# Putting the up product of a feed-forward pair together in PSUM, with its loads and splits placed earlier

## The chip, the core and the metric

The kernel runs on one core of one Trainium2 chip. The metric is the time of one execution on the device, in microseconds (us); lower is better. Several executions are timed and their median is given, and one further execution is profiled. The engines are named as the profile names them: PE (TensorE; PEld is its weight load), DVE (VectorE), ACT (ScalarE), POOL (GpSimd) and SP (SyncE, which here only issues DMAs).

## The reference

Two layers of an encoder over 512 positions of width 1024, in 32-bit floats. Each layer has a mixer (latent attention beside a gated convolution), then a gated MLP with a depthwise convolution of width 3 between its up product and the SiLU, then a gated embedding. The change is in the MLP:

```python
h = rmsnorm(x, g_ffn[i])
u = dwconv(h @ w_up[i], w_ffn_conv[i])
a, val = u[..., :D_FF], u[..., D_FF:]
x = x + (jax.nn.silu(a) * val) @ w_down[i]
```

D_FF is 2816, so `h @ w_up` has 5632 columns. `dwconv` mixes three neighbouring positions of one channel with three weights of its own (its "taps"), zero at both ends.

## The kernel before

Activations of the MLP lie transposed: 128 channels on the partitions, 512 positions along the free axis. Each 32-bit operand of a product is split into a high part (a copy rounded by ACT, `split` or `wsplit`, line 93 or 106) and a low part (the rest, by a DVE subtraction, line 94 or 107), and `mm3` adds three products: high·high (line 101), high·low of the moving side (102) and low·high (103). So each weight tile is loaded by SP into a `raw` buffer, copied by ACT to `wh` (or `vh`) and subtracted by DVE to `wl` (or `vl`).

The feed-forward works in pairs: pair j is one tile of 128 columns of `a` and the matching tile of `val`, in `w_up` tiles 2j and 2j+1. There are 22 pairs in a layer. The first two (`ew`, `eo`) are plain products whose sums stay in four PSUM banks, from which `taps` reads them. The other 20 go through the generator `pair`, which treats the 2x2 blocks (two halves of the positions, two halves of the 1024 input channels, and `a` beside `val`) by a scheme with seven block products of 256 columns in place of eight. Its inputs are sums and differences of blocks: on the moving side the tiles `hf`, `sh`, `sl`, made once per layer on DVE and ACT (lines 580 to 591), on the weight side four POOL subtractions per pair in the two `raw` buffers (lines 614 to 617), after `r0` (blocks b11, b21) has been split as `w0` and the block b22 as `w22` (`vh`, `vl`). After the second of the four, `r1` is split as `w1`; after the fourth, `r0` is split again as `w2`.

`pair` yields between its steps, called s0 to s7 here:

- s0: load `r0`, `r1`; split `w0` and `w22`; the four POOL subtractions
- s1: product y (with `w0`), in the bank "av"
- s2: product x (with `w0`), in a bank "mm"; y is copied to SBUF (`U`) and x + y goes to `C`, an SBUF tile; split `w1`
- s3: product z (with `w1`), in a bank "sc"; split `w2`
- s4: more onto x (with `w2`); x and z are copied to SBUF (`U`, `Z`)
- s5: more onto x (with `w1`); x + Z goes to `C`
- s6: more onto z (with `w22`); z + U goes to `C`
- s7: more onto x (with `w2`); x is copied to `C`; then `taps` on both halves of `C`, and `gated`

Each step's product is twelve matmuls of 256 columns. `taps` is one scaled copy on ACT (line 563) and two multiply-adds on DVE (564, 565); `gated` is the SiLU on ACT (601), a product on DVE (602, `fa` times `fa`) and a split into `gth`, `gtl` (106, 107).

The down product of four finished pairs is cut in eight pieces (`down`): each is twelve matmuls of 512 columns into a bank "tp", with a DVE addition into the residual `xs` (line 539). It loads and splits four `w_down` tiles per four pairs, two ahead of its first piece and two more later.

The main loop interleaves an old pair, a new one and the next one, and the pieces. On PE the order is that of the code (a manual region), and one turn of the loop is: old s4, new s1, piece, old s5, new s2, new s3, piece, old s6, old s7. The other engines are ordered by the framework's scheduler, and each executes its instructions strictly in the order given, so that one that waits holds up all behind it. There are four `raw` buffers, eight each of `wh` and `wl`, two of `vh` and `vl`, and PSUM banks: two "mm", one "av", two "sc", three "tp".

Of the kernel before, what the change touches and what calls it, by code (L numbers as in the profile page):

```python
# [11 lines left out]
F32 = mybir.dt.float32  # L12
# [4 lines left out]
ALU = mybir.AluOpType  # L17
AX = mybir.AxisListType

P = 128  # L20
L = 2
S = 512
# [18 lines left out]
HS = S // 2  # L41
# [19 lines left out]
def encoder_kernel(ctx, tc, x_in, pT, pos, inv, w_a1, w_z, w_g, w_uq, w_ukv, w_au, w_cu, w_o,  # L61
                   w_up, w_down, w_pg, w_ple, b_gate, g_norm, g_lat, g_nope, g_rope, w_conv,
                   w_fconv, out):
    nc = tc.nc
# [7 lines left out]
    hh = cp.tile([P, NT, KD, P], F32R, name="hh")  # L72
    hl = cp.tile([P, NT, KD, P], F32R, name="hl")
# [3 lines left out]
    def psum(tag="mm"):  # L77
        return ps.tile([P, S], F32, tag=tag, name="ps_" + tag, bufs={"mm": 2, "av": 1, "sc": 2, "tp": 3}[tag])
# [5 lines left out]
    def load(src, n=1024):  # L84
        raw = rawtile(n)
        nc.sync.dma_start(raw, src)
        return raw

    def wsplit(raw, n=1024, tag="w"):
        wp, nr, nw = wpool[-1]  # L90
        h = wp.tile([P, n], F32R, tag=tag + "h", name=tag + "h", bufs=nw if tag == "w" else 2)
        lo = wp.tile([P, n], F32R, tag=tag + "l", name=tag + "l", bufs=nw if tag == "w" else 2)
        nc.scalar.copy(h, raw)  # L93
        nc.vector.tensor_sub(lo, raw, h.bitcast(F32))  # L94
        return h, lo
# [4 lines left out]
    def mm3(o, st, mv, start, stop, more=False):  # L100
        nc.tensor.matmul(o, st[0], mv[0], start=start, stop=False, skip_group_check=more)  # L101
        nc.tensor.matmul(o, st[0], mv[1], start=False, stop=False, skip_group_check=more)  # L102
        nc.tensor.matmul(o, st[1], mv[0], start=False, stop=stop, skip_group_check=more)  # L103

    def split(hi, lo, src):
        nc.scalar.copy(hi, src)
        nc.vector.tensor_sub(lo, src, hi.bitcast(F32))  # L107
# [88 lines left out]
    def pool(name, l):  # L196
        cm = tc.tile_pool(name=f"{name}{l}", bufs=1, reuse_waits="tile")
        p = cm.__enter__()
        return p, lambda: cm.__exit__(None, None, None)

    def layer(l, first):
# [67 lines left out]
        def t2(nm):  # L269
            return tmp.tile([P, S], F32, tag="t2", name=nm, bufs=4)  # L270
# [233 lines left out]
        for m in range(KD):  # L504
            gs = []
            for i in range(2):
                w = weight(w_g[l, 2 * m + i])
                o = psum()
# [48 lines left out]
        ff, close_ff = pool("ff", l)  # L557
# [3 lines left out]
        def taps(i, o):  # L561
            a = t2("fa")
            nc.scalar.activation(a, o, AF.Copy, scale=wfc[:, i, 1:2])  # L563
            nc.vector.scalar_tensor_tensor(a[:, 1:], o[:, :-1], wfc[:, i, 0:1], a[:, 1:], ALU.mult, ALU.add)  # L564
            nc.vector.scalar_tensor_tensor(a[:, :-1], o[:, 1:], wfc[:, i, 2:3], a[:, :-1], ALU.mult, ALU.add)  # L565
            return a
# [11 lines left out]
        hf = [ff.tile([P, 2, 4, P], F32, tag="gt", name="hf", bufs=8) for q in quarter]  # L578
        V = nc.vector
        for o, q in zip(hf, quarter):  # L580
            V.tensor_tensor(o, hh[q].bitcast(F32), hl[q].bitcast(F32), ALU.add)
        h11, h12, h21, h22 = hf
        V.tensor_tensor(h22, h22, h21, ALU.add)
        V.tensor_tensor(h21, h21, h11, ALU.subtract)
# [7 lines left out]
        def quart(r, k0):  # L592
            return lambda k: (hh[:, 2 * r:2 * r + 2, k0 + k, :], hl[:, 2 * r:2 * r + 2, k0 + k, :])

        def summed(i):
            return lambda k: (sh[:, i, :, k, :], sl[:, i, :, k, :])
# [3 lines left out]
        def gated(j, u):  # L600
            nc.scalar.activation(u[0], u[0], AF.Silu)
            nc.vector.tensor_tensor(u[1], u[0], u[1], ALU.mult)
            if j % 2 == 0:
                gt[j // 2] = (ff.tile([P, 2, S], F32R, tag="gt", name="gth", bufs=8),
                              ff.tile([P, 2, S], F32R, tag="gt", name="gtl", bufs=8))
            split(gt[j // 2][0][:, j % 2, :], gt[j // 2][1][:, j % 2, :], u[1])

        def pair(j):
            r0, r1 = load(w_up[l, 2 * j]), load(w_up[l, 2 * j + 1])
            b11, b21, b12, b22 = r0[:, :512], r0[:, 512:], r1[:, :512], r1[:, 512:]  # L610
            w0 = wsplit(r0)
            w22 = wsplit(b22, 512, "v")
            g = nc.gpsimd
            g.tensor_tensor(b22, b12, b22, ALU.subtract)  # L614
            g.tensor_tensor(b12, b12, b11, ALU.subtract)  # L615
            g.tensor_tensor(b11, b11, b22, ALU.subtract)  # L616
            g.tensor_tensor(b21, b21, b11, ALU.subtract)
            yield

            def product(o, w, off, mv, first):  # L620
                for k in range(4):
                    c = slice(off + k * P, off + k * P + P)
                    mm3(o, (w[0][:, c], w[1][:, c]), mv(k), first and k == 0, k == 3, not first)

            C = ff.tile([P, 2, S], F32, tag="C", name="C", bufs=2)
            U = ff.tile([P, HS], F32, tag="U", name="U", bufs=2)
            y = psum("av")[:, :HS]
            product(y, w0, 512, quart(0, 4), True)
            yield
            x = psum("mm")[:, :HS]  # L630
            product(x, w0, 0, quart(0, 0), True)
            nc.scalar.copy(U, y)
            V.tensor_tensor(C[:, 0, :HS], x, U, ALU.add)
            w1 = wsplit(r1)
            yield
            z = psum("sc")[:, :HS]
            product(z, w1, 0, summed(0), True)
            w2 = wsplit(r0)
            yield
            product(x, w2, 0, summed(1), False)  # L640
            U = ff.tile([P, HS], F32, tag="U", name="U", bufs=2)
            Z = ff.tile([P, HS], F32, tag="U", name="Z", bufs=2)
            nc.scalar.copy(U, x)
            nc.scalar.copy(Z, z)
            yield
            product(x, w1, 512, quart(1, 0), False)
            V.tensor_tensor(C[:, 1, HS:], x, Z, ALU.add)
            yield
            product(z, w22, 0, summed(2), False)
            V.tensor_tensor(C[:, 1, :HS], z, U, ALU.add)  # L650
            yield
            product(x, w2, 512, quart(1, 4), False)
            nc.scalar.copy(C[:, 0, HS:], x)
            gated(j, [taps(2 * j + i, C[:, i, :]) for i in range(2)])

        def down(j0, j1, after, tags):
            nk = (j1 - j0) // 2

            def tiles(n):
                return [weight(w_down[l, n * (NJ // 2) + j0 // 2 + k]) for k in range(nk)]  # L660

            wt = tiles(0)
            for n in range(2):
                for t in range(NT):
                    yield
                    tk = slice(t * P, (t + 1) * P)
                    o = psum(tags[t % len(tags)])
                    for i in range(2 * nk):
                        h, lo = gt[j0 // 2 + i // 2]
                        wh, wl = wt[i // 2]  # L670
                        c = slice((i % 2) * 512, (i % 2) * 512 + 512)
                        mm3(o, (h[:, i % 2, tk], lo[:, i % 2, tk]), (wh[:, c], wl[:, c]), i == 0, i == 2 * nk - 1)
                    after(t, n, o)
                    if n == 0 and t == 2:
                        nxt = tiles(1)
                if n == 0:
                    wt = nxt
# [3 lines left out]
        def piece():  # L681
            while downs and next(downs[0], downs) is downs:
                downs.pop(0)

        def advance(g, n=1):
            for _ in range(n if g else 0):
                next(g, None)
# [3 lines left out]
        region = tc.manual_schedule(engines={mybir.EngineType.PE})  # L691
        region.__enter__()
        old, new = None, pair(NS)
        advance(new)
        for q in range(NS, NJ + 1):
            nxt = pair(q + 1) if q + 1 < NJ else None
            advance(old)
            advance(new)
            piece()
            advance(old)  # L700
            advance(new, 2)
            advance(nxt)
            piece()
            advance(old, 2)
            if old and q % 4 == 0:
                downs.append(down(q - 4, q, residual, ("tp",)))
            old, new = new, nxt
# [45 lines left out]
    for l in range(L):  # L753
        layer(l, l == 0)
# [79 lines left out]
```

## Time and profile before

| | |
|---|---|
| median of 3 runs | 1644.79 us (1640.87 to 1645.81) |
| the profiled execution | 1645.68 us |
| its span, first to last instruction | 1643.8 us |
| busy in the span | PE 94%, PEld 82%, DVE 71%, ACT 49%, POOL 22% |
| mean granted clock of PE | 0.975 |
| first product of the 20 pairs, first and second layer | at 396 us and 1212 us of the span |

The page gives shares over the whole span; the change touches only the feed-forward of each layer, so that its price is read from views cut to those stretches: the instructions in order of time, the waits of PE, and the windows. A matmul counts as busy until its modelled end, which lies after the start of the next ones; the pace of PE is read from starts.

### The profile page before, as it was taken

The numbers are of one execution on the slowest core, as the hardware profiler recorded it, in microseconds if no ns is written. First come the engines' busy times: TensorE is split into PE (matmuls) and PEld (weight loads), VectorE is DVE, ScalarE is ACT, GpSimd is POOL, SyncE is SP. The second block draws the span as 40 slices with busy tenths as digits, with TensorE's granted clock in tenths as the row PEclk, the third lists the DMA queues.
The fourth block names the chain that finished last, engine by engine and source line by source line (L and its number), as shares of the span: only waits on it lengthen the run. The fifth ranks groups of instructions, "written<-read, shape, count | busy, mean of one in ns | idle before, by whom it ended". The sixth has DMA issues, their size and how long they took to land.

```text
span 1643.8 us, 22339 instructions
## 1 busy us (share of the span) xinstructions
PE 1542.8 (94%) x8776; PEld 1344.5 (82%) x8776; DVE 1162.6 (71%) x1500; ACT 805.0 (49%) x1336; POOL 364.5 (22%) x313
## 2 busy tenths in 40 slices
PE   7999999988899989999989999999788999999998
PEld 6888888868788878887888888888687888888876
DVE  7787543359789898887367775433688889889862
ACT  6588632234444544555264885332345454455541
POOL 2700000003343343411045000000034334343110
PEclk9999999998899999999999999999898999999999
DMA  6220223213223323243042112322222332323411
GB/s 213 73 65 26 84 87 99 79 64 103 78 78 92 113 78 103 78 152 90 21 138 77 39 39 78 102 91 66 79 89 78 91 104 88 103 77 100 152 51 45
DMA packets 41448, 142.32 MB, mean 87 GB/s; under 512 B 5760, under 2 KB 6272, under 8 KB 41344
## 3 DMA queue, kind: packets, MB, share of 16 engines
q1 hardware_dynamic: 41344, 140.90, 27.8%
q8 instruction: 69, 1.13, 0.3%
q14 instruction: 35, 0.29, 0.1%
HBM read 138.78 MB, written 2.10 MB: 86 GB/s over the span
## 4 chain that ended last, share of the span: by engine, by line
PE 43%; DVE 17%; issue 8%; ACT 3%; DMA 3%; POOL 1%; DVEq 0%; ACTq 0%; POOLq 0%; SPq 0%
PE ps_mm L101 6%; PE ps_mm L103 6%; PE ps_mm L102 6%; DVE fa L565 5%; PE ps_sc L103 5%; DVE fa L564 4%; PE ps_sc L101 4%; PE ps_sc L102 4%; DVE wl L94 4%; DMA raw<-in_w_down_dram 3%; PE ps_tp L103 3%; PE ps_tp L101 2%; PE ps_tp L102 2%; ACT wh L93 1%; DVE xs L539 1%
## 5 line engine op out<-in xcount | busy, mean ns | idle before, releaser
L93 ACT CAST wh<-raw 128x1024 fp32r<-128x1024 f32 (+1 forms) x290 | 297.9, 1045 | 393.3 <-PE ps_mm L102 85.1
L94 DVE TENSOR_TENSOR wl<-raw,wh 128x1024 fp32r<-128x1024 f32 (+1 forms) x290 | 372.9, 1290 | 149.9 <-ACT wh L93 148.4
L101 PE MATMUL ps_mm<-hh,wh 128*128 128x256 f32 (+1 forms) x992 | 337.0, 340 | 4.3 <-ACT wh L93 3.2
L103 PE MATMUL ps_mm<-hh,wl 128*128 128x256 f32 (+1 forms) x992 | 332.5, 335 | 5.8 <-DVE wl L94 5.8
L102 PE MATMUL ps_mm<-hl,wh 128*128 128x256 f32 (+1 forms) x992 | 332.4, 335 | 0.0
L103 PEld LDWEIGHTS ps_mm<-hh,wl 128*128 128x128 f32 x992 | 189.0, 191 | 26.4 <-DVE wl L94 6.4
L101 PEld LDWEIGHTS ps_mm<-hh,wh 128*128 128x128 f32 x992 | 189.3, 191 | 24.8 <-ACT wh L93 3.9
L102 PEld LDWEIGHTS ps_mm<-hl,wh 128*128 128x128 f32 x992 | 189.6, 191 | 18.9
L111 POOL TENSOR_SCALAR ms<-ms 128x1 f32<-128x1 f32 (+2 forms) x40 | 14.3, 356 | 750.6 <-ACT junk L130 722.5
L614 POOL TENSOR_TENSOR raw<-raw 128x512 f32<-128x512 f32 x40 | 62.4, 1560 | 427.4 <-DVE vl L94 427.4
L565 DVE SCALAR_TENSOR_TENSOR fa<-C,wfc,fa 128x511 f32<-128x511 f32 x80 | 131.1, 1675 | 0.0
L103 PE MATMUL ps_tp<-wh,gtl 128*128 128x512 f32 x320 | 128.0, 400 | 1.6 <-DVE gtl L107 1.6
L101 PE MATMUL ps_tp<-wh,gth 128*128 128x512 f32 x320 | 128.9, 403 | 0.0
L102 PE MATMUL ps_tp<-wl,gth 128*128 128x512 f32 x320 | 128.6, 402 | 0.0
L564 DVE SCALAR_TENSOR_TENSOR fa<-C,wfc,fa 128x511 f32<-128x511 f32 x80 | 93.9, 1213 | 24.4 <-ACT fa L563 24.4
L103 PE MATMUL ps_sc<-sh,wl 128*128 128x256 f32 x160 | 51.9, 324 | 48.0 <-DVE wl L94 48.0
L103 PEld LDWEIGHTS ps_sc<-sh,wl 128*128 128x128 f32 x160 | 34.5, 216 | 52.2 <-DVE wl L94 52.2
L103 PEld LDWEIGHTS ps_tp<-wh,gtl 128*128 128x128 f32 x320 | 61.5, 192 | 18.1 <-DVE gtl L107 3.3
L101 PEld LDWEIGHTS ps_tp<-wh,gth 128*128 128x128 f32 x320 | 62.1, 194 | 11.7
L102 PEld LDWEIGHTS ps_tp<-wl,gth 128*128 128x128 f32 x320 | 61.7, 193 | 11.4
L615 POOL TENSOR_TENSOR raw<-raw 128x512 f32<-128x512 f32 x40 | 70.1, 1754 | 2.9
L616 POOL TENSOR_TENSOR raw<-raw 128x512 f32<-128x512 f32 x40 | 67.6, 1689 | 10.0 <-issue 3.6
(291 smaller groups left out, 3676.2 us busy)
## 6 DMA issues: line engine op xcount, KB each, us to landing
raw<-in_w_up_dram SPq DMA_DIRECT2D x88, 512.0 KB, 3.7
raw<-in_w_down_dram SPq DMA_DIRECT2D x44, 512.0 KB, 3.7
raw<-in_w_g_dram SPq DMA_DIRECT2D x32, 512.0 KB, 3.6
raw<-in_w_z_dram SPq DMA_DIRECT2D x24, 512.0 KB, 3.8
raw<-in_w_o_dram SPq DMA_DIRECT2D x16, 512.0 KB, 3.7
raw<-in_w_pg_dram SPq DMA_DIRECT2D x16, 512.0 KB, 3.6
raw<-in_w_au_dram SPq DMA_DIRECT2D x8, 512.0 KB, 3.7
raw<-in_w_cu_dram SPq DMA_DIRECT2D x8, 512.0 KB, 3.6
```

The source lines that it names most:

```text
L93: nc.scalar.copy(h, raw)
L94: nc.vector.tensor_sub(lo, raw, h.bitcast(F32))
L101: nc.tensor.matmul(o, st[0], mv[0], start=start, stop=False, skip_group_check=more)
L102: nc.tensor.matmul(o, st[0], mv[1], start=False, stop=False, skip_group_check=more)
L103: nc.tensor.matmul(o, st[1], mv[0], start=False, stop=stop, skip_group_check=more)
L111: nc.gpsimd.tensor_scalar_add(ms, ms, EPS)
L539: nc.vector.tensor_tensor(xs[:, t, c], xs[:, t, c], o, ALU.add)
L564: nc.vector.scalar_tensor_tensor(a[:, 1:], o[:, :-1], wfc[:, i, 0:1], a[:, 1:], ALU.mult, ALU.add)
L565: nc.vector.scalar_tensor_tensor(a[:, :-1], o[:, 1:], wfc[:, i, 2:3], a[:, :-1], ALU.mult, ALU.add)
L614: g.tensor_tensor(b22, b12, b22, ALU.subtract)
L615: g.tensor_tensor(b12, b12, b11, ALU.subtract)
L616: g.tensor_tensor(b11, b11, b22, ALU.subtract)
```

## The change

The sums of a pair no longer go to the SBUF tile `C`. The product x is put in the right half of an "mm" bank (`m0`), and x + y is written by DVE into the left half; z is put in the left half of an "sc" bank (`m1`), x + Z is written into its right half, and z + U is added in place. `taps` then reads `m0` and `m1` in PSUM. The ACT copy of the last x to `C` is gone. Both banks are held until the taps have read them. `U`, `Y` and `Z` share four small SBUF buffers.

The split of `w1` is placed behind s1 instead of s2 and that of `w2` behind s2 instead of s3, and the next pair's s0 now stands between the new pair's s2 and s3. The order of the products on PE is the same. Once per layer, the four additions that make `hf` go from DVE to POOL.

```diff
         for o, q in zip(hf, quarter):
-            V.tensor_tensor(o, hh[q].bitcast(F32), hl[q].bitcast(F32), ALU.add)
+            nc.gpsimd.tensor_tensor(o, hh[q].bitcast(F32), hl[q].bitcast(F32), ALU.add)
...
-            C = ff.tile([P, 2, S], F32, tag="C", name="C", bufs=2)
-            U = ff.tile([P, HS], F32, tag="U", name="U", bufs=2)
+            def side(nm):
+                return ff.tile([P, HS], F32, tag="U", name=nm, bufs=4)
+
             y = psum("av")[:, :HS]
             product(y, w0, 512, quart(0, 4), True)
-            yield
-            x = psum("mm")[:, :HS]
-            product(x, w0, 0, quart(0, 0), True)
-            nc.scalar.copy(U, y)
-            V.tensor_tensor(C[:, 0, :HS], x, U, ALU.add)
             w1 = wsplit(r1)
             yield
-            z = psum("sc")[:, :HS]
-            product(z, w1, 0, summed(0), True)
+            m0 = psum("mm")
+            x = m0[:, HS:]
+            product(x, w0, 0, quart(0, 0), True)
+            Y = side("Y")
+            nc.scalar.copy(Y, y)
+            V.tensor_tensor(m0[:, :HS], x, Y, ALU.add)
             w2 = wsplit(r0)
             yield
+            m1 = psum("sc")
+            z = m1[:, :HS]
+            product(z, w1, 0, summed(0), True)
+            yield
             product(x, w2, 0, summed(1), False)
-            U = ff.tile([P, HS], F32, tag="U", name="U", bufs=2)
-            Z = ff.tile([P, HS], F32, tag="U", name="Z", bufs=2)
+            U, Z = side("U"), side("Z")
             nc.scalar.copy(U, x)
             nc.scalar.copy(Z, z)
             yield
             product(x, w1, 512, quart(1, 0), False)
-            V.tensor_tensor(C[:, 1, HS:], x, Z, ALU.add)
+            V.tensor_tensor(m1[:, HS:], x, Z, ALU.add)
             yield
             product(z, w22, 0, summed(2), False)
-            V.tensor_tensor(C[:, 1, :HS], z, U, ALU.add)
+            V.tensor_tensor(z, z, U, ALU.add)
             yield
             product(x, w2, 512, quart(1, 4), False)
-            nc.scalar.copy(C[:, 0, HS:], x)
-            gated(j, [taps(2 * j + i, C[:, i, :]) for i in range(2)])
+            gated(j, [taps(2 * j, m0), taps(2 * j + 1, m1)])
...
             advance(old)
-            advance(new, 2)
+            advance(new)
             advance(nxt)
+            advance(new)
             piece()
```

What the scheduler makes of it on DVE, in a turn of the loop of the first layer, from the split of `w1` to the last addition of the old pair. Before (L94 is a weight split, L602 to L107 the gated product and its split, L539 the residual of a down piece, L647, L633 and L650 the additions into `C`):

```order
L94 TENSOR_TENSOR wl_4675<-raw_4523,wh_4674 128x1024
L602 TENSOR_TENSOR fa_4581<-fa_4577,fa_4581 128x512
L539 TENSOR_TENSOR xs_67<-xs_67,ps_tp_4620 128x512
L94 TENSOR_TENSOR wl_4692<-raw_4521,wh_4691 128x1024
L647 TENSOR_TENSOR C_4443<-ps_mm_4485,Z_4602 128x256
L94 TENSOR_TENSOR wl_4700<-raw_4695,wh_4699 128x1024
L107 TENSOR_TENSOR gtl_4424<-fa_4581,gth_4423 128x512
L633 TENSOR_TENSOR C_4605<-ps_mm_4659,U_4606 128x256
L539 TENSOR_TENSOR xs_67<-xs_67,ps_tp_4711 128x512
L650 TENSOR_TENSOR C_4443<-ps_sc_4504,U_4601 128x256
```

The same turn in the changed kernel (`raw_4498` is r1, `raw_4496` r0, `raw_4668` the next pair's r0, and `raw_4623` and `raw_4629` are `w_down` tiles; the additions are now L650, L637 and L653):

```order
L94 TENSOR_TENSOR wl_4606<-raw_4498,wh_4605 128x1024
L94 TENSOR_TENSOR wl_4626<-raw_4623,wh_4625 128x1024
L539 TENSOR_TENSOR xs_67<-xs_67,ps_tp_4609 128x512
L94 TENSOR_TENSOR wl_4632<-raw_4629,wh_4631 128x1024
L602 TENSOR_TENSOR fa_4568<-fa_4564,fa_4568 128x512
L650 TENSOR_TENSOR ps_sc_4512<-ps_mm_4476,Z_4589 128x256
L94 TENSOR_TENSOR wl_4665<-raw_4496,wh_4664 128x1024
L637 TENSOR_TENSOR ps_mm_4648<-ps_mm_4648,Y_4661 128x256
L94 TENSOR_TENSOR wl_4673<-raw_4668,wh_4672 128x1024
L107 TENSOR_TENSOR gtl_4413<-fa_4568,gth_4412 128x512
L539 TENSOR_TENSOR xs_67<-xs_67,ps_tp_4697 128x512
L653 TENSOR_TENSOR ps_sc_4512<-ps_sc_4512,U_4588 128x256
```

In every fourth turn, as in this one, two splits of `w_down` tiles now stand right behind that of `w1`, and the split of the gated product (`gtl`) has moved from seventh to tenth place, behind the split of the next pair's first tile. In two of the other turns no `w_down` split stands at all, and in one two stand behind `gtl`; before, two stood behind `gtl` in every second turn.

The other place is the start of the feed-forward, on DVE, where the last rows of the normalisation (`hl` from `ps_tp`), the splits of the first four tiles and the sums `hf` meet. Before:

```order
L581 TENSOR_TENSOR hf_3524<-hh_68,hl_69 128x1024
L581 TENSOR_TENSOR hf_3525<-hh_68,hl_69 128x1024
L581 TENSOR_TENSOR hf_3526<-hh_68,hl_69 128x1024
L107 TENSOR_TENSOR hl_69<-ps_tp_3284,hh_68 128x512
L94 TENSOR_TENSOR wl_3305<-raw_3302,wh_3304 128x1024
L581 TENSOR_TENSOR hf_3527<-hh_68,hl_69 128x1024
L94 TENSOR_TENSOR wl_3311<-raw_3308,wh_3310 128x1024
L583 TENSOR_TENSOR hf_3527<-hf_3527,hf_3526 128x1024
```

In the changed kernel DVE has this:

```order
L107 TENSOR_TENSOR hl_69<-ps_tp_3284,hh_68 128x512
L94 TENSOR_TENSOR wl_3305<-raw_3302,wh_3304 128x1024
L94 TENSOR_TENSOR wl_3311<-raw_3308,wh_3310 128x1024
L94 TENSOR_TENSOR wl_3317<-raw_3314,wh_3316 128x1024
L94 TENSOR_TENSOR wl_3323<-raw_3320,wh_3322 128x1024
L583 TENSOR_TENSOR hf_3527<-hf_3527,hf_3526 128x1024
```

and POOL has the four sums between the last step of the normalisation's root (L112) and the first subtractions of the first pair:

```order
L112 TENSOR_TENSOR rs1_3270<-ms_3268,negh_71 128x1
L581 TENSOR_TENSOR hf_3524<-hh_68,hl_69 128x1024
L581 TENSOR_TENSOR hf_3525<-hh_68,hl_69 128x1024
L581 TENSOR_TENSOR hf_3526<-hh_68,hl_69 128x1024
L581 TENSOR_TENSOR hf_3527<-hh_68,hl_69 128x1024
L614 TENSOR_TENSOR raw_3576<-raw_3576 128x512
```

The splits of the first four weight tiles now follow the normalisation directly, and the first sum of two quarters (L583) stands behind all four of them and behind POOL.

## The prediction

> **What bounds the kernel now.** The page's first part, then the waits of PE over the whole span (what waited, for whom: us in total, times, longest):
>
> ```profile
> PE 1542.8 (94%) x8776; PEld 1344.5 (82%) x8776; DVE 1162.6 (71%) x1500; ACT 805.0 (49%) x1336; POOL 364.5 (22%) x313
> PE ps_sc L103 <- DVE wl L94: 48.0, 20, 4.3
> PE ps_mm L101 <- DVE C L633: 10.6, 4, 6.1
> ```
>
> PE is the bound on average, and its largest wait is the third matmul of z (s3) for the low part of `w1` from DVE: 48 us, 20 times, in 40 pairs. So the loop is where time can be had. What PE itself needs for a turn, from three starts in its order of time:
>
> ```profile
> 490.40 0.40 PE L101 MATMUL ps_tp<-wh,gth 128*128 128x512 f32 x1
> 493.20 0.28 PE L101 MATMUL ps_mm<-hh,wh 128*128 128x256 f32 x1
> 496.05 0.28 PE L101 MATMUL ps_sc<-sh,wh 128*128 128x256 f32 x1
> ```
>
> The twelve matmuls of a down piece take 2.80 us (0.233 each), the 24 of s5 and s2 2.85 us (0.119 each). A turn has seven products and two pieces: 84 x 0.119 + 24 x 0.233 = 9.98 + 5.60 = 15.6 us. What it takes, from the chain that ended last, which passes the first taps of a pair:
>
> ```profile
> 453.76 2.45 DVE fa L564 x2
> 523.09 2.45 DVE fa L564 x2
> 591.03 2.45 DVE fa L564 x2
> 659.47 2.45 DVE fa L564 x2
> ```
>
> Twelve turns in 205.7 us: 17.1 us each, and 68.0 and 68.4 for four, against 62.4 on PE alone. So 1.5 us of a turn is waiting. Where, in PE's order of time, from 505 to 592:
>
> ```profile
> 514.17 0.39 PE L103 MATMUL ps_sc<-sh,wl 128*128 128x256 f32 x1 [1.65 <-DVE wl L94]
> 518.58 0.50 PE L103 MATMUL ps_tp<-wh,gtl 128*128 128x512 f32 x1 [0.40 <-DVE gtl L107]
> 548.35 0.39 PE L103 MATMUL ps_sc<-sh,wl 128*128 128x256 f32 x1 [2.23 <-DVE wl L94]
> ```
>
> It is every second turn, at z. Behind that stands DVE (and POOL, ACT) in the turn from 506, in order of time:
>
> ```profile
> 506.05 2.44 DVE L564 SCALAR_TENSOR_TENSOR fa<-C,wfc,fa 128x511 f32<-128x511 f32 x2
> 508.42 3.48 DVE L565 SCALAR_TENSOR_TENSOR fa<-C,wfc,fa 128x511 f32<-128x511 f32 x2
> 511.82 2.29 DVE L94 TENSOR_TENSOR wl<-raw,wh 128x1024 fp32r<-128x1024 f32 x1
> 506.21 1.74 POOL L614 TENSOR_TENSOR raw<-raw 128x512 f32<-128x512 f32 x1 [11.97 <-DVE vl L94]
> 508.03 1.62 POOL L615 TENSOR_TENSOR raw<-raw 128x512 f32<-128x512 f32 x1
> 509.68 1.05 ACT L93 CAST wh<-raw 128x1024 fp32r<-128x1024 f32 x1 [2.85 <-POOL raw L615]
> ```
>
> The high part of `w1` is done at 510.73, but its low part starts at 511.82, behind four taps of 5.85 us, and ends at 514.1, when PE goes on. The turn itself is late because ACT stands before a `w_down` tile whose buffer was freed late:
>
> ```profile
> 496.00 4.76 DMA raw<-in_w_down_dram
> ```
>
> **The change, part by part.** *Taps from PSUM.* The view of lines 564 and 565 gives min/median/max by source, and the first pairs' taps, which read PSUM, ran in part beside POOL:
>
> ```profile
> L564 DVE SCALAR_TENSOR_TENSOR fa<-C,wfc,fa x80: 744/752/1791, 419.7 to 1556.9; 128x511 f32<-128x511 f32 x80
> L565 DVE SCALAR_TENSOR_TENSOR fa<-C,wfc,fa x80: 743/1780/1790, 422.1 to 1559.3; 128x511 f32<-128x511 f32 x80
> L565 DVE SCALAR_TENSOR_TENSOR fa<-ps_mm,wfc,fa x4: 737/748/750, 393.0 to 1221.7; 128x511 f32<-128x511 f32 x4
> 390.03 2.31 DVE L107 TENSOR_TENSOR sl<-hf,sh 128x1024 fp32r<-128x1024 f32 x1
> 392.26 0.73 DVE L564 SCALAR_TENSOR_TENSOR fa<-ps_mm,wfc,fa 128x511 f32<-128x511 f32 x1
> 391.22 2.27 POOL L617 TENSOR_TENSOR raw<-raw 128x512 f32<-128x512 f32 x1
> L614 POOL TENSOR_TENSOR raw<-raw x40: 1288/1725/2278, 380.7 to 1525.7; 128x512 f32<-128x512 f32 x40
> ```
>
> Beside POOL an SBUF subtraction takes 2.31 us, and a tap from SBUF up to 1.79; the tap from PSUM that began inside the POOL instruction at 391.22 took 0.73. POOL's own 128x512 goes from 1.29 to 2.28. So four taps cost 4 x 0.74 = 3.0 us in place of 5.85, and POOL's first two come to 2.6 instead of 3.4. By the Trainium skill, "SBUF — State Buffer", section "Who interferes with whom", a DVE instruction with at most one SBUF input does not contend with GpSimd and one with two does, exclusively; the rows above agree, and a tap from PSUM has one.
>
> What is late next: in a turn that starts at 0 (start of s4) z is wanted at 3 x 1.43 + 2.80 + 1.43 = 8.5 us. The two subtractions end at about 2.8 to 3.1, ACT's copy (1.05, behind the copy of y, whose product ends at 2.9) at 4.4, and the low part of `w1`, now itself beside POOL and so at 2.3, at 6.7: 1.8 us to spare. Freed 1 to 2 us earlier, the `raw` buffers let the `w_down` loads and the splits behind them start earlier too. The wait at z goes: 2.5 us per two turns.
>
> *What moves.* The next pair's s0 is issued ahead of s3: two loads on SP, the splits of `w0` and `w22`, four POOL instructions. On SP the sequence of up and down loads stays the same, and on POOL that of the subtractions after the start, so this moves only places on ACT and DVE; they are counted where they matter, below.
>
> *New waits.* The banks are held until the last tap. The next x in the same bank starts at 7.1 in the turn; taps end near 4, or 5 in a turn whose `vl` is 2 us late: nothing. The Trainium skill, "PSUM — Partial Sum Buffer", section "Terms", calls PE writing and another engine on one bank at once a collision, which would speak against writing sums beside an open product. Here the semaphores order them (s6 waits for X+Z, done near 10.7, and begins at 12.8), so no run before shows it and the sum stays. The additions write PSUM, for which no row exists; the nearest is the same addition into SBUF:
>
> ```profile
> L633 DVE TENSOR_TENSOR C<-ps_mm,U x40: 407/415/425, 406.3 to 1540.2; 128x256 f32<-128x256 f32 x40
> 523.00:591.00 68.00, 62.96 (x435) 57.85 (x434) 60.35 (x64) 33.62 (x54) 25.91 (x17) 1.00 0.32 93
> ```
>
> I take 0.42; between 0.3 and 0.75 (a tap of twice the width) three of them move DVE by -0.4 to +1.0 us per turn. DVE (60.35 in the window of four turns) is busy 15.1 us per turn now and would be 15.1 - 2.85 = 12.3, plus some 1.2 for the slowed split, of 15.6: either end still fits. The ACT copy that goes (0.37) was not on the chain.
>
> The `gtl` split is what I expect to become late: in the fourth turn it stands behind two `w_down` splits and the next r0, whose load can start only when `w1`'s low part frees its buffer (6.7, some 4.5 of load: 11.2, copy 12.2, split 13.5), so `gtl` ends near 14.2. The piece that needs it begins at 9.95, and its twelfth matmul at 12.5: a wait of 1.7 us per four turns, 0.4 now. Four turns: 62.4 + 1.7 = 64.1, instead of 68.4 (17.1 x 4). Gain 1.1 us per turn, for the 15 turns from the fourth to the nineteenth of the 20 pairs **16.5 us per layer**. The last turns have one more wait at z (PE's waits from 710 to 740):
>
> ```profile
> PE ps_sc L103 <- DVE wl L94: 2.4, 1, 2.4
> ```
>
> Of it I count 1.
>
> *The first turns.* The second and third wait at z too, and PE's granted clock falls (the third figure from the end of a window's row):
>
> ```profile
> 426.75 0.38 PE L103 MATMUL ps_sc<-sh,wl 128*128 128x256 f32 x1 [2.27 <-DVE wl L94]
> 443.31 0.58 PE L103 MATMUL ps_sc<-sh,wl 128*128 128x256 f32 x1 [4.31 <-DVE wl L94]
> 409.00:454.00 45.00, 38.23 (x268) 36.74 (x268) 31.18 (x35) 20.27 (x34) 14.87 (x10) 0.87 0.25 71
> ```
>
> Without a piece ahead of it z is wanted at 5.7, `w1` comes near 6.6: of 4.3 and 2.3 us some 0.9 each stay. That is 4.8, and a third of the 45 x 0.13 = 5.9 us that the clock withheld: 1.9. Together **6.7**.
>
> *`hf` on POOL.* Start of the feed-forward, first layer:
>
> ```profile
> 362.40 1.41 DVE L135 SCALAR_TENSOR_TENSOR ht<-xs,rs,gbc 128x512 f32<-128x512 f32 x2
> 365.64 3.49 DVE L581 TENSOR_TENSOR hf<-hh,hl 128x1024 f32<-128x1024 f32 x3
> 373.05 1.22 DVE L583 TENSOR_TENSOR hf<-hf 128x1024 f32<-128x1024 f32 x1
> 401.24 0.36 PE L101 MATMUL ps_sc<-sh,wh 128*128 128x256 f32 x1 [2.68 <-ACT fa L563]
> 406.80 0.38 PE L101 MATMUL ps_mm<-sh,wh 128*128 128x256 f32 x1 [3.92 <-DVE C L633]
> ```
>
> DVE gives up 4 x 1.14 = 4.6 us, but POOL needs 4 x 2.6 (twice 1.29), in order, from 362.3; each SBUF instruction of DVE in that time (two `ht`, two or three splits) waits for one of them, and each of them for one of DVE. Alternating with five of DVE (0.7 to 1.14, mean 0.9): 362.3 + 4 x 2.6 + 5 x 0.9 = 377.2 for the last sum and, after the last splits, 378.5 for L583, now 373.05. So the chain to the first pair is 5.5 us late, and the waits at 401 and 406 end that much later: **-5.5** per layer, between -8 (the clock falls again) and 0 (if the taps' banks were the wait, not this chain).
>
> Sum per layer: 16.5 + 1 + 6.7 - 5.5 = 18.7, for two 37. From the profiled execution, 1645.7 - 37 = 1608.7; the median lies 0.9 lower: **1608**.
>
> **The rivals.** *All waits of the loop go* (the `gtl` wait too, if the load of the next r0 is shorter than I took): 15 x 1.5 + 2.5 + 9 - 5.5 = 28.5 per layer: 1588. For it: DVE has 2 us to spare per turn. Against it: the order of rows with `gtl` last.
>
> *The split chain stays the pace.* Turns with late `w_down` loads push `vl` and so the next `w1` past 8.5, every second turn loses 1.7 more and `gtl` another 0.5: gain 0.5 per turn, 7.5 + 0.5 + 4 - 5.5 = 6.5 per layer: 1632. For it: the load of 4.76 us and ACT standing before it.
>
> *Taps do not get faster* (the side that is slower): if a tap from PSUM were slowed beside POOL as one from SBUF, the loop keeps its 17.1, x waits 0.2 for its bank in every second turn (taps to 494.8 against 494.6), the first turns keep theirs, and the `hf` price remains: 2 x (5.5 + 1.5) = 14: 1659. It decides at a tap of (7.1 - 1.4) / 4 = 1.4 us. Against it: 0.73 beside POOL.
>
> *It is hidden anyway*: a DVE order as full as before, with the split beside POOL taking what the taps give (2 x 1.1 us per turn), ends with gain and `hf` price equal: 1644.
>
> **How the numbers follow.** Forecast 0.57 (1597 to 1622); all waits go 0.14; split chain 0.15; no faster taps 0.08; hidden 0.06. The range leaves out the last two and the edges: 1585 to 1638. About 0.3% (5 us) is what a measurement can tell from no change: faster 0.86, same 0.06, slower 0.08.
>
> **What would show it.** In the new profile: L564 and L565 at 0.74 throughout; no wait of PE at z for `wl` in steady turns; a wait at `ps_tp` for `gtl` near 1.7 us every fourth; turns of 15.6 to 16; L583 near 378.5. Wrong would be taps above 1.4 us, turns of 17, or PE waiting for taps ahead of x (L101 `ps_mm` for `fa`).

## The result, and the profile after

| | before | after |
|---|---|---|
| median, timed together | 1645.3 us (1640.87 to 1647.86, 4 runs) | 1598.41 us (1594.93 to 1599.05, 4 runs) |
| ratio, 95% interval | | 0.9713 [0.9688, 0.9739] |
| span of the profiled execution | 1643.8 us | 1597.3 us |
| mean granted clock of PE | 0.975 | 0.984 |
| first product y of the 20 pairs, by layer | 395.6 and 1212.3 us | 397.6 and 1189.3 us |

The kernel is 2.9% faster, by 46.9 us at the medians and 46.5 us in the spans. First the line of busy times on the page and the shares of the chain that ended last:

```profile
PE 1529.9 (96%) x8776; PEld 1333.6 (83%) x8776; DVE 1065.9 (67%) x1492; ACT 788.1 (49%) x1296; POOL 347.7 (22%) x321
...
PE 80%; DVE 8%; issue 4%; ACT 3%; POOL 3%; DMA 2%; SPq 0%; DVEq 0%; POOLq 0%; ACTq 0%
```

The last chain of the kernel before had PE at 43% and DVE at 17%; now PE has four fifths of it. DVE is busy 97 us less. The waits of PE over the whole span (us in total, times, longest) say what is left:

```profile
PE ps_tp L138 <- DVE ht L135: 22.2, 7, 7.3
PE ps_mm L101 <- DVE ps_mm L637: 9.2, 2, 4.6
PE ps_tp L103 <- DVE gtl L107: 7.2, 8, 1.0
PE ps_sc L101 <- DVE fa L565: 6.1, 2, 3.1
...
PE ps_sc L103 <- DVE wl L94: 4.2, 4, 1.5
```

The wait at z for the split of `w1` fell from 48.0 us in 20 places to 4.2 in 4, all in the first turns. In its place stands the wait of a down piece for `gtl`, 7.2 us in 8 places. The rows with L637 and L565 (first pairs), and 6.9 us per layer of the row with `ht` (normalisation; 3.2 before), belong to the start of the feed-forward, where the sums `hf` are.

The same two layers, cut by the starts of the products y (the first matmul into the bank "av" of each pair):

| stretch | before, us | after, us | gained |
|---|---|---|---|
| layer 1, to the second pair's y | 409.2 | 412.6 | -3.4 |
| second to fifth pair | 44.6 | 36.5 | 8.1 |
| fifth to twentieth pair, 15 turns | 254.6 | 236.6 | 18.0 |
| to the first y of layer 2 | 503.9 | 503.6 | 0.3 |
| layer 2, first to second pair | 13.3 | 15.0 | -1.7 |
| second to fifth pair | 44.2 | 36.6 | 7.6 |
| 15 turns | 254.1 | 238.9 | 15.2 |
| to the end | 119.9 | 117.5 | 2.4 |

The taps and the new additions, grouped by source line (ns, min/median/max; first and last start):

```profile
L564 DVE SCALAR_TENSOR_TENSOR fa<-ps_mm,wfc,fa x44: 734/749/753, 393.0 to 1508.7; 128x511 f32<-128x511 f32 x44
L565 DVE SCALAR_TENSOR_TENSOR fa<-ps_sc,wfc,fa x44: 736/742/750, 402.8 to 1512.5; 128x511 f32<-128x511 f32 x44
L637 DVE TENSOR_TENSOR ps_mm<-ps_mm,Y x40: 418/423/433, 409.4 to 1489.8; 128x256 f32<-128x256 f32 x40
L653 DVE TENSOR_TENSOR ps_sc<-ps_sc,U x40: 423/432/433, 421.2 to 1505.6; 128x256 f32<-128x256 f32 x40
L614 POOL TENSOR_TENSOR raw<-raw x40: 1287/1295/5085, 384.2 to 1478.5; 128x512 f32<-128x512 f32 x40
```

No tap is above 0.753 us; before, the median of line 565 was 1.78. An addition that ends in PSUM takes 0.42 to 0.43 us, where the one into SBUF took 0.415. POOL's first subtraction is 1.295 us in the median, and was 1.725.

A fourth turn, where the new wait stands, in order of time (start, duration, engine, line, tile; in brackets the idle time before and what ended it):

```profile
495.12 0.75 DVE L564 SCALAR_TENSOR_TENSOR fa<-ps_mm,wfc,fa 128x511 f32<-128x511 f32 x1 [0.92 <-ACT fa L563]
...
497.10 0.74 DVE L565 SCALAR_TENSOR_TENSOR fa<-ps_sc,wfc,fa 128x511 f32<-128x511 f32 x1
498.65 3.27 DVE L94 TENSOR_TENSOR wl<-raw,wh 128x1024 fp32r<-128x1024 f32 x2 [0.81 <-ACT wh L93]
...
504.51 1.21 DVE L94 TENSOR_TENSOR wl<-raw,wh 128x1024 fp32r<-128x1024 f32 x1
505.64 0.42 DVE L637 TENSOR_TENSOR ps_mm<-ps_mm,Y 128x256 f32<-128x256 f32 x1
505.97 1.21 DVE L94 TENSOR_TENSOR wl<-raw,wh 128x1024 fp32r<-128x1024 f32 x1
507.11 0.68 DVE L107 TENSOR_TENSOR gtl<-fa,gth 128x512 fp32r<-128x512 f32 x1
494.28 1.29 POOL L614 TENSOR_TENSOR raw<-raw 128x512 f32<-128x512 f32 x1 [10.10 <-DVE vl L94]
497.56 2.95 ACT L93 CAST wh<-raw 128x1024 fp32r<-128x1024 f32 x3
504.53 1.05 ACT L93 CAST wh<-raw 128x1024 fp32r<-128x1024 f32 x1 [2.54 <-DMA raw<-in_w_up_dram]
507.85 0.50 PE L103 MATMUL ps_tp<-wh,gtl 128*128 128x512 f32 x1 [0.95 <-DVE gtl L107]
```

The window of the four turns after it (length, then busy PE, PEld, DVE, ACT and POOL, then the granted clock, DMA share, GB/s):

```profile
512.00:576.00 64.00, 62.97 (x440) 58.20 (x439) 50.96 (x66) 32.29 (x50) 22.15 (x18) 1.00 0.32 99
```

The taps end at 497.84 (497.10 + 0.74), 2.7 us after they began. The split of `w1`, the first of the two at 498.65, waits for ACT's copy alone and no longer for taps. What is late is `gtl`, at the end of DVE's row: the load of the next pair's r0 lands at 504.5 and its copy ends at 505.58, but DVE reaches its split only at 505.97, behind the split of `w2` (504.51) and L637 (505.64). That split ends at 507.18, `gtl` behind it at 507.79, and PE has waited 0.95. The chain that ended last stays on DVE from 500.71, the first split of a `w_down` tile, to the end of `gtl`. In the window DVE is busy 50.96 of 64 us, and the clock is whole.

### The profile page after: what moved, and what is told of

It is laid out like the page before. It is cut to its first block, busy times and chain, and to the rows that moved or that the text cites. A ratio compares the mean times of both kernels' runs of the same rounds, so it can differ in the third digit from the quotient of the medians.

```text
span 1597.3 us, 22350 instructions
## 1 busy us (share of the span) xinstructions
PE 1529.9 (96%) x8776; PEld 1333.6 (83%) x8776; DVE 1065.9 (67%) x1492; ACT 788.1 (49%) x1296; POOL 347.7 (22%) x321
## 4 chain that ended last, share of the span: by engine, by line
PE 80%; DVE 8%; issue 4%; ACT 3%; POOL 3%; DMA 2%; SPq 0%; DVEq 0%; POOLq 0%; ACTq 0%
PE ps_mm L101 12%; PE ps_mm L103 12%; PE ps_mm L102 12%; PE ps_sc L103 7%; PE ps_sc L101 7%; PE ps_sc L102 7%; PE ps_tp L103 4%; DVE wl L94 4%; PE ps_tp L102 4%; PE ps_tp L101 4%; PE ps_av L101 2%; PE ps_av L103 2%; PE ps_av L102 2%; PE ps_tp L442 2%; ACT wh L93 1%
## 5 line engine op out<-in xcount | busy, mean ns | idle before, releaser
L94 DVE TENSOR_TENSOR wl<-raw,wh 128x1024 fp32r<-128x1024 f32 (+1 forms) x290 | 380.6, 1321 | 173.4 <-ACT wh L93 171.7
L614 POOL TENSOR_TENSOR raw<-raw 128x512 f32<-128x512 f32 x40 | 61.3, 1534 | 394.7 <-DVE vl L94 394.7
L93 ACT CAST vh<-raw 128x512 fp32r<-128x512 f32 x40 | 24.9, 622 | 120.0 <-PE ps_sc L102 117.3
L539 DVE TENSOR_TENSOR xs<-xs,ps_tp 128x512 f32<-128x512 f32 x80 | 54.5, 681 | 23.3 <-PE ps_tp L103 23.2
L617 POOL TENSOR_TENSOR raw<-raw 128x512 f32<-128x512 f32 x40 | 60.0, 1501 | 3.0
L112 POOL TENSOR_TENSOR rs<-ms,negh 128x1 f32<-128x1 f32 (+2 forms) x40 | 56.1, 1402 | 3.1
L135 DVE SCALAR_TENSOR_TENSOR ht<-xs,rs,gbc 128x512 f32<-128x512 f32 x48 | 42.1, 915 | 21.8 <-POOL rs L112 14.5
L101 PE MATMUL ps_mm<-sh,wh 128*128 128x256 f32 x160 | 46.2, 289 | 9.2 <-DVE ps_mm L637 9.2
```

The source lines that it names most:

```text
L112: nc.gpsimd.tensor_tensor(r, ms, negh[:, :n], ALU.pow)
L135: nc.vector.scalar_tensor_tensor(ht, xs[:, t, c], r, g[:, c], ALU.mult, ALU.mult)
L539: nc.vector.tensor_tensor(xs[:, t, c], xs[:, t, c], o, ALU.add)
```

## The experiments

Each kernel was timed beside the kernel before, which took 1642.4 us beside e1 to e4, 1643.1 beside e5 to e8, 1645.2 beside e9 and e10, and 1645.3 beside the changed kernel. A difference between two kernels that were not timed side by side can therefore be some 3 us off; where it matters, the difference by the two ratios to the kernel before is given as well. "e3", "e8" and so on stand for the runs below.

**e1: the sums in PSUM alone.** Splits, loads and the order of the loop stand as before, and `hf` is on DVE. The edit is of the changed kernel.

```diff
-nc.gpsimd.tensor_tensor(o, hh[q].bitcast(F32), hl[q].bitcast(F32), ALU.add)
+V.tensor_tensor(o, hh[q].bitcast(F32), hl[q].bitcast(F32), ALU.add)
...
 product(y, w0, 512, quart(0, 4), True)
-w1 = wsplit(r1)
...
 V.tensor_tensor(m0[:, :HS], x, Y, ALU.add)
-w2 = wsplit(r0)
+w1 = wsplit(r1)
...
 product(z, w1, 0, summed(0), True)
+w2 = wsplit(r0)
...
-advance(new)
+advance(new, 2)
 advance(nxt)
-advance(new)
```

> The kernel before with one part of the change: the sums of a pair are put together in the two PSUM banks and the taps read them there; the splits of w1 and w2, the next pair's first step and the four sums hf stay where they were before. Contention theory (a tap with both inputs in SBUF is held up by POOL, one with an input in PSUM is not, and that alone frees the split of w1): taps at 0.74 us, no wait of PE at z in steady turns, turns of 15.6 to 16 us, and without the price of hf at the start (3.4 us per layer in the changed kernel) 1590 to 1600. Order theory (the earlier splits free the raw buffers and that is the gain): above 1630.

Measured: 1579.47 us (1578.36 to 1581.4), ratio 0.9625 [0.961, 0.9639]. This part alone gains more than the whole change. One row of the taps by source line:

```profile
L564 DVE SCALAR_TENSOR_TENSOR fa<-ps_mm,wfc,fa x44: 736/749/751, 392.2 to 1490.0; 128x511 f32<-128x511 f32 x44
```

And the waits of PE at the places in question:

```profile
PE ps_sc L103 <- DVE wl L94: 3.0, 4, 1.0
...
PE ps_tp L103 <- DVE gtl L107: 1.4, 2, 1.1
```

The wait at z goes from the steady turns without any split being moved, these turns are 15.5 us, and the wait for `gtl` comes twice instead of eight times. This part also holds the loss of the ACT copy of the last x (0.37 us per pair), which no run separates from the taps; before the change ACT's copy of `w1` was done 1.1 us before DVE came to split it, so that it was not ACT that was late.

**e2: the earlier splits and loads alone.** The sums go to `C` as before, `hf` is on DVE. The edit is of the kernel before.

```diff
 product(y, w0, 512, quart(0, 4), True)
+w1 = wsplit(r1)
...
 V.tensor_tensor(C[:, 0, :HS], x, U, ALU.add)
-w1 = wsplit(r1)
+w2 = wsplit(r0)
...
 product(z, w1, 0, summed(0), True)
-w2 = wsplit(r0)
...
-advance(new, 2)
+advance(new)
 advance(nxt)
+advance(new)
```

> The kernel before with the other part: w1 split behind s1, w2 behind s2, the next pair's first step ahead of s3; the sums stay in C in SBUF and hf on DVE. Contention theory: the taps still take 5.8 us of each turn beside POOL, the low part of w1 still stands behind them, 1635 to 1645. Order theory: below 1605.

Measured: 1638.85 us, ratio 0.9977 [0.9964, 0.999]. The waits of PE:

```profile
PE ps_sc L103 <- DVE wl L94: 25.0, 12, 2.6
PE ps_tp L101 <- ACT gth L106: 13.3, 8, 2.5
PE ps_tp L103 <- DVE gtl L107: 5.3, 8, 0.9
```

And one row of the taps by source line:

```profile
L565 DVE SCALAR_TENSOR_TENSOR fa<-C,wfc,fa x80: 736/1780/1786, 422.3 to 1552.6; 128x511 f32<-128x511 f32 x80
```

The wait at z is halved (48.0 to 25.0), but 18.6 us of waiting for `gth` and `gtl` stand where 1.6 us stood before. Turns still alternate between 15.5 and about 18 us. As long as the taps take 1.78 us, another order only moves the late instruction.

**e3 and e7: the sums `hf`.** e3 is the changed kernel with `hf` on DVE, e7 the kernel before with `hf` on POOL.

```diff
-nc.gpsimd.tensor_tensor(o, hh[q].bitcast(F32), hl[q].bitcast(F32), ALU.add)
+V.tensor_tensor(o, hh[q].bitcast(F32), hl[q].bitcast(F32), ALU.add)
```

> The changed kernel with the four sums hf back on DVE. If the sums on POOL hold up DVE and the chain to the first pair: first product back from 397.6 to about 395.6, second product 3.4 us earlier, and the same in the second layer: 1591 to 1593. If the waits at the start come from the taps' banks, whoever makes the sums: 1598, no difference.

> The kernel before with only the four sums hf on POOL. From the sums put back (10 us faster): slower by 4 to 10 us, 1647 to 1653, with first products 2 us later and second ones 3.4 us later than before. If the price of the sums is only there beside taps from PSUM: no difference.

Measured: e3 1588.36 us, ratio 0.9678 [0.9663, 0.9694], 10.0 us below the changed kernel (5.8 by the ratios) and 3 us below what was expected. e7 1654.34 us, ratio 1.0066 [1.0044, 1.0088], 11.3 above the kernel before, beside which it was timed, and 1 us above what was expected. From both sides, with other taps and another order, the move of `hf` costs time: 5.6 us per layer by e7, 2.9 to 5.0 by e3. In the trace of the changed kernel, start of the feed-forward, layer 1:

```profile
362.52 5.45 DVE L135 SCALAR_TENSOR_TENSOR ht<-xs,rs,gbc 128x512 f32<-128x512 f32 x2
362.33 5.09 POOL L581 TENSOR_TENSOR hf<-hh,hl 128x1024 f32<-128x1024 f32 x2
370.81 6.86 DVE L94 TENSOR_TENSOR wl<-raw,wh 128x1024 fp32r<-128x1024 f32 x4 [0.25 <-ACT wh L93]
368.65 5.67 POOL L581 TENSOR_TENSOR hf<-hh,hl 128x1024 f32<-128x1024 f32 x2 [1.23 <-DVE hl L107]
377.60 1.21 DVE L583 TENSOR_TENSOR hf<-hf 128x1024 f32<-128x1024 f32 x1
```

The two `ht` that took 1.41 us together now take 5.45, about as long as two sums on POOL (5.09), and PE waits for the normalisation that comes from them. The last sum on POOL ends at 374.32, but L583 begins only at 377.60 (373.05 before), behind the last of the four weight splits, which took 6.86 us. In e3 the second pair's y is back at 409.3 (412.6 with the sums on POOL, 409.2 before), and the three turns behind it take 35.4 and 35.2 us by layer, with a granted clock of 0.99 and 1.00, against 36.5 and 36.6 at 0.96 in the changed kernel.

**e4: every down piece one place later,** in the changed kernel, so that the piece that needs a new `gtl` comes after it.

```diff
             wt = tiles(0)
+            if j0 == 0:
+                yield
             for n in range(2):
```

> The changed kernel with every down piece from the first on one place later in PE's order (the first of four pairs' pieces then begins in the turn after the one that makes its last gtl). If the 1.3 us that PE loses in every fourth turn are the split gtl alone: these eight waits go, turns of 15.5 throughout, 1588 to 1592. If the w_down splits take over as the wait: a wait of PE at ps_tp for wl in their place, 1596 to 1600.

Measured: 1581.64 us, ratio 0.9635 [0.9621, 0.965], 16.8 us below the changed kernel (12.8 by the ratios) and 6 us below what was expected. Its waits of PE have no row for `gtl`. All turns but the first few are 15.5 us (16.8 for every fourth before this edit, and one of 19.2), and the turn from the fourth pair to the fifth, which now holds one piece less, falls from 14.5 to 11.7. That turn had not been counted in the expectation; the stretches behind the last pair did not grow for it by as much (502.4 us against 503.6 in layer 1, 118.8 against 117.5 in layer 2).

**e5: the kernel before without the four POOL subtractions of a pair.** The taps read SBUF, and nothing else of the pair is touched.

```diff
-            g.tensor_tensor(b22, b12, b22, ALU.subtract)
-            g.tensor_tensor(b12, b12, b11, ALU.subtract)
-            g.tensor_tensor(b11, b11, b22, ALU.subtract)
-            g.tensor_tensor(b21, b21, b11, ALU.subtract)
```

> The kernel before without the four POOL subtractions of a pair, so w1 and w2 are split from the loaded blocks themselves and the up product is not the reference's; the sums stay in C in SBUF. Contention theory: with POOL silent the taps from SBUF take 0.75 us at most, all 80 of each line, and PE's waits at z go: below 1605. If reading C from SBUF were slow in itself: taps stay at 1.2 and 1.7 on average.

Measured: 1561.03 us, one time only. By source line:

```profile
L564 DVE SCALAR_TENSOR_TENSOR fa<-C,wfc,fa x80: 742/745/751, 414.6 to 1472.3; 128x511 f32<-128x511 f32 x80
L565 DVE SCALAR_TENSOR_TENSOR fa<-C,wfc,fa x80: 737/744/749, 415.9 to 1474.8; 128x511 f32<-128x511 f32 x80
```

All 160 taps from SBUF take what a tap from PSUM takes, while the additions into `C` and the place of the tile are as before. It is neither `C` nor SBUF as such that is slow, but SBUF beside a busy POOL. The time itself is no measure of the taps, since the chain through the subtractions is gone as well.

**e6: half of it.** In the changed kernel the `val` half is assembled in an SBUF tile; the `a` half stays in its PSUM bank.

```diff
-V.tensor_tensor(m1[:, HS:], x, Z, ALU.add)
+C = ff.tile([P, S], F32, tag="C", name="C", bufs=2)
+V.tensor_tensor(C[:, HS:], x, Z, ALU.add)
...
-V.tensor_tensor(z, z, U, ALU.add)
+V.tensor_tensor(C[:, :HS], z, U, ALU.add)
...
-gated(j, [taps(2 * j, m0), taps(2 * j + 1, m1)])
+gated(j, [taps(2 * j, m0), taps(2 * j + 1, C)])
```

> The changed kernel, but with the second tile of a pair (val) put together in C in SBUF as before and only the first (a) in PSUM. Two taps at 0.74 and two from SBUF beside POOL at up to 1.8: some 4.4 us, the low part of w1 about 1.4 us later than in the changed kernel, at 8.1 of the 8.5 us at which z wants it. Contention theory with that slack: 1598 to 1606, next to nothing lost. If the gain goes with the time of the taps: half way, 1615 to 1625.

Measured: 1604.82 us, ratio 0.9766 [0.9745, 0.9787]. The taps by source line:

```profile
L564 DVE SCALAR_TENSOR_TENSOR fa<-ps_mm,wfc,fa x44: 733/749/751, 393.2 to 1513.4; 128x511 f32<-128x511 f32 x44
L564 DVE SCALAR_TENSOR_TENSOR fa<-C,wfc,fa x40: 740/1702/1716, 422.5 to 1514.0; 128x511 f32<-128x511 f32 x40
L565 DVE SCALAR_TENSOR_TENSOR fa<-C,wfc,fa x40: 740/1124/1129, 424.8 to 1517.1; 128x511 f32<-128x511 f32 x40
```

The waits of PE:

```profile
PE ps_sc L103 <- DVE wl L94: 6.7, 4, 2.2
PE ps_tp L103 <- DVE gtl L107: 7.0, 8, 1.1
PE ps_tp L101 <- ACT gth L106: 4.8, 8, 1.1
```

Within one kernel, beside the same POOL instructions, the taps from PSUM keep 0.749 and those from SBUF take 1.70 and 1.12. Three turns of four are still 15.5 us and the fourth 17.5 instead of 16.8: in steady turns the split of `w1` has enough to spare for two slow taps. What they cost appears where something was late already, at `gth` and `gtl` and at z in the first turns (6.7 us instead of 4.2). The gain does not go in proportion to the taps.

**e8: e3 and e4 together.**

> The changed kernel with the sums back on DVE and every down piece one place later. If the two prices are separate they add: 1598.4 - 10 - 16.8 = 1571 to 1574. If the later piece gives its gain only by covering the late start of the first pairs: 1578 to 1582, no better than either.

Measured: 1575.54 us (1574.69 to 1576.1), ratio 0.9588 [0.957, 0.9607]. The time lies between the two expectations. The two savings, 10.0 and 16.8, give 22.9 together (5.8 and 12.8 give 20.6 by the ratios), so they add within what can be told, and the later piece does more than cover the late start. From the sixth pair every turn is 15.5 us.

**e9: the sums in PSUM and the pieces one place later, with nothing else of the change** (e1 with the edit of e4), **and e10: e8 again on the same chip.**

> The sums assembled in PSUM, with the splits, the loads and the sums of the quarters where the kernel before has them, and every down piece one place later. Theory (the earlier splits and loads of the change bring nothing once the taps read PSUM; they only make the split of the gated product late): the steady turns are 15.5 us here as well, the last product of PE is reached as early as in the kernel that has the earlier splits too, and the time is 1573 to 1579. Rival (the earlier splits are worth their place once the pieces stand later, in the first turns, where z comes without a piece ahead of it): waits at z for the split of w1 come back in the first turns (2 to 4 us per layer), and the time is 1580 to 1585.

> The kernel with everything of the change but the sums of the quarters on DVE, and the pieces one place later, again on the same chip as the one above, so that the two are compared by runs of one call: 1574.5 to 1576.5 by its first four runs. If the other lies within 5 us of it, the earlier splits and loads are worth nothing that can be told here.

Measured: e9 1580.74 us, ratio 0.9611 [0.9597, 0.9626]; e10 1576.12 us, 0.9583 [0.9567, 0.9599]. Neither theory has it. The time lies where the rival put it, but its waits at z did not come: 2.9 us in 4 places in e9, 3.9 in 4 in e10. The steady turns are 15.5 us in both, as the theory said. Of the 3.2 us between the two spans, 1.1 lies between the first and the last y of layer 1 (280.9 against 279.8 us), and 3.1 between there and the first y of layer 2 (501.9 against 498.8); in the rest e9 is the shorter by 1.0 (0.4 ahead of the first y, 0.2 in the loop of layer 2, 0.4 behind it). Of the 3.1 us, 2.2 are one wait of PE in the mixer that follows, which e10 lacks:

```profile
PE ps_sc L101 <- ACT qc L330: 2.2, 1, 2.2
```

So once the pieces stand later, the earlier splits are worth 1 us in the loop of one layer and nothing in that of the other. Why that copy in the next mixer is late in some of these kernels (the kernel before and the changed one have a wait of 1.9 us there) stays open. And the pieces one place later bring nothing that can be told without the earlier splits (ratio 0.9625 in e1, 0.9611 in e9), where `gtl` was late only twice.

## Why the prediction was right

Forecast 1608, range 1585 to 1638; measured 1598.4. The mechanism is the one predicted: e5 and e6 show that the taps were slow because of POOL and are not slow from PSUM, and e1 that this alone takes the wait at z away. By its steps:

- *Taps 0.74 us, the addition into PSUM 0.42*: measured 0.742 to 0.749 and 0.422 to 0.432 in the medians. The Trainium skill's "SBUF — State Buffer", section "Who interferes with whom", is borne out by two runs for this instruction: without POOL's subtractions (e5) two SBUF inputs cost nothing, and with POOL busy (e6) only those with two SBUF inputs are slowed.
- *DVE 12.3 us per turn, plus up to 1.2*: 12.7 (50.96 / 4). *PE alone 15.6*: 15.5.
- *Four turns in 64.1, a wait of 1.7 for `gtl` in the fourth*: 63.4 (from 512.4 to 575.8), with 0.95 of idle time, a turn of 16.8. The place, its engine and its rhythm were right, the reason only in part. The load of the next r0, taken to land 11.2 us into the turn, landed at 10.3 (504.5, in a turn whose s4 starts at 494.2), and what came last was not the load but DVE's own row. Only in one turn of layer 2, the one of 19.2 us that the forecast did not have, does the last chain go through the load (4.77 us from 1356.04); there PE waited 1.0 us for `gth` and 0.6 for `gtl`, and its granted clock was 0.50 in the 3.4 us behind that. The 15 turns of a layer gained 18.0 and 15.2 us; 16.5 was predicted.
- *First turns 6.7*: 8.1 and 7.6. Waits at z stay, 2.2 and 2.1 us by layer where 1.8 was predicted; they were 6.6 and 6.7. The term was too small in what the clock gives back, counted as 1.9. The same turns of layer 1 in the changed kernel, with the clock third from the end (0.87 before), are these:

```profile
412.60:449.10 36.50, 34.34 (x266) 33.33 (x266) 26.07 (x35) 19.14 (x31) 11.46 (x9) 0.96 0.26 87
```

Reckoned as in the prediction, the clock withheld 44.6 x 0.13 = 5.8 us before and 36.5 x 0.04 = 1.5 now: by this estimate it gave back 4.3.

- *`hf` -5.5*: by the runs -2.9 to -5.0 (e3) and -5.6 (e7), with L583 at 377.6 (378.5 predicted). That this moment was met is in part luck: the sums on POOL were done at 374.3 and not at 377.2, and the weight splits on DVE held L583 instead. In the trace -3.4 and -3.7 are seen up to the second pair's y (the latter with the 2.0 us that the first y is late in layer 1 taken for layer 2); the rest appears behind it, where e3, with a clock of 0.99 and 1.00, takes 1.1 and 1.4 us less from the second pair to the fifth.
- *The last turns 1*: 2.3 to 2.4 per layer, the end of layer 2 directly and that of layer 1 if the late start of the next layer's first y is taken as there.

The sum was 37 us and 46.5 came. The mis-sized terms are the first turns (1.2 per layer), the last (1.4 per layer), and the price of `hf` as this one trace shows it (about 2 per layer). The largest term was right to 0.1 us in the mean of the layers, 16.6 against 16.5, and that is luck in part: both sides of it were taken too long, 15 turns before at 256.5 us (254.6 and 254.1 measured) and after at 240.4 (236.6, and 238.9 with the turn of 19.2).

Of the rivals, *all waits of the loop go* is not what happened, but it is what e4 makes of the kernel, where pieces one place later take the wait for `gtl` out. *The split chain stays the pace* is refuted by the absence of any wait at z in steady turns, *taps do not get faster* by every tap, and *hidden anyway* by DVE's 12.7 us.

What the prediction did not ask is which parts of the change are needed. The order part, with slow taps, is worth 0.2% (e2). With fast taps it costs 8.9 us (e1 1579.5 against e3 1588.4). It puts `gtl` behind two `w_down` splits and that of the next r0, and PE waits 6.9 us for `gtl` in e3 instead of 1.4; of the 6.4 us between the two spans the loops show 3.1, and the rest, ahead of them and behind, stays open. With the pieces one place later that is mended, and the order is worth some 4.6 us (e10 against e9), of which the loops show 1. The fastest of the kernels that leave nothing out, e8, has the sums in PSUM, the earlier splits, `hf` on DVE and the pieces one place later: 1575.5 us against 1598.4 for the change as it was made.

## What to carry to other kernels

- When an engine in front of the bound one is late, look first at whether its instructions take what they take alone. Here a tap took up to 1.79 us instead of 0.74 because POOL was busy in SBUF, and taking one operand from PSUM was worth 63.0 us where reordering around the slow taps was worth 3.6 (e1 and e2, against the 1642.4 of the kernel before beside them).
- A strictly ordered engine has a last place, and moving instructions up moves another down. Before a split is placed earlier, look at which one it passes, who needs that, and whether its own input has landed; or move the consumer, as e4 does.
- Work given to an engine that is idle on average (POOL, 22%) can cost more than it frees, when both engines then read SBUF at the same time on the path that starts a stage.

## What the runs showed that was not expected

The price of `hf` on POOL was worked out on the supposition that DVE and POOL take turns in SBUF, one instruction each. Before the change they do so in the start of the feed-forward: from 383.3 to 392 us each row of DVE on SBUF takes 2.31 or 2.32 and, from 384.5 on, each of POOL 2.27 or 2.28 (the rows at 390.03 and 391.22 in the prediction are two of them). In the changed kernel, at the same place, they do not. DVE and POOL in order of time:

```profile
383.99 1.22 DVE L586 TENSOR_TENSOR hf<-hf 128x1024 f32<-128x1024 f32 x1
385.13 1.22 DVE L107 TENSOR_TENSOR sl<-hf,sh 128x1024 fp32r<-128x1024 f32 x1
386.26 0.69 DVE L94 TENSOR_TENSOR vl<-raw,vh 128x512 fp32r<-128x512 f32 x1
386.86 1.22 DVE L107 TENSOR_TENSOR sl<-hf,sh 128x1024 fp32r<-128x1024 f32 x1
384.16 5.08 POOL L614 TENSOR_TENSOR raw<-raw 128x512 f32<-128x512 f32 x1 [9.84 <-DVE vl L94]
389.32 1.29 POOL L615 TENSOR_TENSOR raw<-raw 128x512 f32<-128x512 f32 x1
```

POOL began inside a DVE instruction, and then took 5.08 us for what takes it 1.29, while DVE ran four instructions back to back at their undisturbed 1.22 and 0.69. POOL's subtraction ended 1.2 us after the last of them, about as long as it takes alone. Layer 2 shows the same (5.08 us from 1175.93). So POOL can be held for several instructions of DVE, and an estimate by turns can miss that.

Which engine was in SBUF first does not decide it. In the trace of e7 POOL's first subtraction begins at 384.27, 0.16 us into the L586 of 384.11, as it does here 0.17 us into the L586 of 383.99; there it took 2.22 us and the next DVE instruction 2.33, and the two took turns. What does decide stays open.
